# Dense relative-bias tables from the host, built with 16 transfers in place of 64, and the third modulation part accumulated at its place in the queue

## The chip, the core and the metric

The kernel runs on one core of a Trainium2 chip. The metric is the device time of one execution in microseconds, as the median of several executions. Engines are named as in the profile: PE (TensorE matmul), PEld (its weight load), DVE (VectorE), ACT (ScalarE), POOL (GpSimd), SP (SyncE, which issues most DMAs; SPq in rows).

## The reference, cut to what matters

Two transformer layers over 1024 grid tokens (16 rows of 64 columns) and 256 context tokens, width 1024. Layer 0 has 8 neighbourhood-attention heads and 8 grouped-query heads on one input projection; layer 1 is differential attention. Every layer has six modulation vectors per condition, and a SwiGLU FFN.

```python
m = jax.nn.silu(cond) @ w + b                 # six parts: sh1, sc1, g1, sh2, sc2, g2
h = modulate(rms_norm(x), sh1, sc1)           # h * (1 + scale) + shift
...
col_bias = rpb[:, :, col_idx - cols[:, None] + (WIN_C - 1)]
bias = jnp.take(col_bias, row_off, axis=1)    # 15 row offsets x 31 column offsets per head
s_win = einsum(q_r, k_win) * scale + bias     # 8 rows x 16 columns around the query
p = softmax(concat([s_win, s_ctx]))           # plus the 256 context keys
...
x = x + g1 * y
x = x + g2 * swiglu(modulate(rms_norm(x), sh2, sc2), ...)
```

The condition vectors are two: one for the latent tokens, one for the context tokens. The neighbourhood bias of a head is used dense over 64 key columns and 64 query columns, with -1e30 outside the 16-column window.

## The kernel before, in words

Every matmul on activations and weights is done in three passes of split operands (`mm3`, L181 to L183: high by high, low by high, high by low). `load_w` (L171 to L173) loads a weight chunk on SP, makes the high part on ACT and the low part on POOL or DVE.

**The first stage of layer 0**, where the change lies, runs up to the first attention matmul. After norm and the grouped-query projections it has two loops: the V projection (L665, two groups `g` of 10 token tiles) and the plain projections (L719, `ch` 0 to 7: 4 chunks of q, then 4 of k; each is 3 blocks of 24 matmuls into `psm` buffers, of which there are 4). `put_plain` (L360 to L364) evacuates each block on ACT and DVE, and the finished chunk is stored to DRAM (L729, L730).

Into both loops the program weaves side work:

- `maxima` (L408): for each head the row maxima of the scores, which the softmax uses later. A grouped-query head has 26 products (`qk`, L436) into `psq` buffers, of which there are 3, each followed by one DVE reduction (L414), and one transpose (L475). `early` (L650) hands out 200 steps of this over the two loops; the rest runs beside the attention.
- `tables(i, h)` (L626): eight calls, for `i` in (key table, query table) and four pairs of heads. Each does two parts: two broadcast loads of a row of the bias to 64 partitions (L634), one POOL add of the column mask `cmt` (L635), two stores to the DRAM table `sk` (L638). A row of the table has 127 columns, so that `skew` (L151) can read the 64 wanted ones of each row offset from a shifted start. `key_table` (L797, L798; tile TT) and `query_tables` (L813, L814; TQ, TG) read these rows back, in runs of 64 floats.
- the modulation vectors: `ada_acc` (L203) loads eight 128x1024 blocks of one of the six parts (`aw`, L207) and accumulates them for both conditions on DVE (2 x L210, then 14 x L214). `ada_sum` (L230) sums over partitions with 16 single-column matmuls (L235) into a `psq` buffer and adds the bias (L238). Three parts are done here, (0,2), (0,3) and (0,4): summed at the head of V group 1, after chunk 1, and after chunk 4.

The tile `aw` has 3 buffers, and the tables use the same tag: loads of table parts and of modulation blocks take turns in them, in the program's order.

**The order of the work.** A list scheduler puts the instructions of each engine in one fixed order; on the chip each engine and each DMA queue works in that order and waits at its head. `later()` (L298) lowers the priority of what it encloses by 3000, so that it falls behind other ready work. Table calls and all three `ada_acc` stand under `later()`.

Behind the first stage comes the attention of layer 0 (heads 8 to 15, then 0 to 7): `operands` loads q, k and V of each head (L770 to L788), `attend` makes the scores (L857, L858 into `pst`), the probabilities (ACT L847, L852, DVE L850, POOL and DVE L853) and the products with V (L892 to L895 into `psv`). Then follow output projection, FFN, and layer 1.

Of the kernel before, what the change touches and what calls it, by code (L numbers as in the profile page):

```python
# [9 lines left out]
F32 = mybir.dt.float32  # L10
# [7 lines left out]
P = 128  # L18
# [5 lines left out]
NFF = 22  # L24
EPS = 1e-6
GW = 64
RPW = 127
RPN = 15 * RPW
NEG = -1e30
LATER = 3000  # L30
AHEAD1 = 0.25
# [18 lines left out]


@with_exitstack
def kernel(ctx: ExitStack, tc: tile.TileContext, xT, cond, ada_w, ada_b, win0, wv0, wout0, rp, rpf, qg, kg,
                       win1, wv1, wout1, wg, wu, wd, lamv, subln, fgain, cosT, sinT, consts, cmT, cmQ, out):
    nc = tc.nc
    f = lambda ap: ap.bitcast(F32)
    uid = [0]

    def nm(s):
        uid[0] += 1  # L60
        return f"{s}_{uid[0]}"
# [15 lines left out]
    def order(a, b):  # L77

        tc.add_manual_dep(b.ins, a.ins.name, mybir.DependencyInfo(mybir.DependencyClass.NoSync, mybir.DependencyReason.DATA),
                          reason="activation table")  # L80
# [36 lines left out]
    def dram(shape, name):  # L117
        return dpool.tile(shape, F32, name=name)
# [10 lines left out]
    ls1 = dram([8, 2, 2, 8, P], "ls1")  # L129
    xs = dram([KD, P, NX], "xs")  # L130
    onesrow = dram([2, NT], "onesrow")
    sk = [dram([8, 64 * RPN + 2048], f"sk{i}") for i in range(2)]

    def small_operands():
        nc.sync.dma_start(slt, subln)
# [13 lines left out]
        nc.vector.tensor_scalar(slt, slt, 1.0 - LAMBDA_INIT, None, op0=ALU.mult)  # L149

    def skew(i, h, dr0, n):  # L151
        o = 63 + dr0 * RPW
        v = sk[i][h, o : o + 64 * (RPN - 1)].rearrange("(c n) -> c n", c=64)
        return v[:, : n * RPW].rearrange("c (u y) -> c u y", y=RPW)[:, :, :GW]


    pq = [None]
# [18 lines left out]
    def load_wchunk(src, eng=None):  # L176
        hi, lo = load_w(src, eng=eng, view=("p (k m) -> p k m", dict(k=KD)))
        return hi.rearrange("p (k m) -> p k m", k=KD), lo.rearrange("p (k m) -> p k m", k=KD)
# [6 lines left out]
    def project(o, w, hh, hl, ks=tuple(range(KD)), between=None):  # L185
        for i, k in enumerate(ks):
            mm3(o, w[0][:, k, :], w[1][:, k, :], hh[k], hl[k], k == ks[0], k == ks[-1])
            if between:
                between((i + 1) / len(ks))
# [13 lines left out]
    def ada_acc(pool, l, mod, conds, behind=None):  # L203
        acc = [pool.tile([P, 1024], F32, tag="acc", bufs=2, name=nm("acc")) for _ in range(conds)]
        for k in range(KD):
            w = pool.tile([P, 1024], F32, tag="aw", bufs=3, name=nm("aw"))
            nc.sync.dma_start(w, ada_w[l, k, :, mod * 1024 : (mod + 1) * 1024])  # L207
            for c in range(conds):
                if k == 0:
                    ins = nc.vector.tensor_scalar(acc[c], w, cs[:, k, c : c + 1], None, op0=ALU.mult)  # L210
                    if behind:
                        order(behind, ins)
                else:
                    nc.vector.scalar_tensor_tensor(acc[c], w, cs[:, k, c : c + 1], acc[c], op0=ALU.mult, op1=ALU.add)  # L214
        return l, mod, acc
# [82 lines left out]
    def later():  # L298

        return tc.high_priority(-LATER)  # L300
# [82 lines left out]
    def t5(pool, dt=F32R):  # L383
        return pool.tile([P, NT], dt, tag="t5", bufs=T5[0], name=nm("t5"))
# [104 lines left out]
    with sbuf("hp0", 8) as hp, sbuf("a10", 8) as ap:  # L489
# [31 lines left out]
        adas = [(0, 2, 2), (0, 3, 2), (0, 4, 2)]  # L521
# [86 lines left out]
        for g in range(2):  # L608
            w1 = load_wchunk(win0[8 + 2 * g], None if g else nc.vector)
            w2 = load_wchunk(win0[9 + 2 * g], None if g else nc.vector)  # L610
            o = [(t5(tpool), t5(tpool)) for _ in range(2)]
# [8 lines left out]
            for blk in BLK0:  # L620
                if g == 0:
                    gqa_k(wk, hi, lo, blk)
                gqa_q(g, w1, w2, o, blk)
        cmt = ap.tile([P, 2, RPW], F32, tag="cmt", bufs=1, name="cmt")

        def tables(i, h):  # L626

            for d0, d1 in ((0, 8), (8, 15)):
                n = d1 - d0
                T = ap.tile([P, 8, RPW], F32, tag="aw", bufs=3, name=nm("sk"))[:, 0:n, :]  # L630
                T2 = T.rearrange("p u y -> p (u y)")
                for j in range(2):
                    src = (rpf, rp)[i][h + j : h + j + 1, d0 * RPW : d1 * RPW].to_broadcast([64, n * RPW])
                    nc.sync.dma_start(T2[64 * j : 64 * j + 64], src)  # L634
                nc.gpsimd.tensor_add(T, T, cmt[:, i : i + 1, :].to_broadcast([P, n, RPW]))  # L635
                for j in range(2):
                    dst = sk[i][h + j, : 64 * RPN].rearrange("(c n) -> c n", c=64)[:, d0 * RPW : d1 * RPW]
                    nc.sync.dma_start(dst, T2[64 * j : 64 * j + 64])  # L638

        mpool = None  # L640
        tabs8 = [(i, h) for h in range(0, 8, 2) for i in range(2)]
# [1 line left out]
        def next_tables():  # L643
            with later():
                tables(*tabs8.pop(0))
# [4 lines left out]
        def early(x):  # L650

            nonlocal done0
            while done0 < EARLY0 * x and next(side0, "end") != "end":
                done0 += 1
# [6 lines left out]
        with later():  # L661
            pend_ada = ada_acc(ap, *adas.pop(0), last_sub[0])
        tok = [(0, i * P) for i in range(2)] + [(1, i * P) for i in range(4)] + [(2, i * P) for i in range(4)]

        for g, (v0, vw, pr0) in enumerate(((0, 384, 0), (384, 256, 3))):  # L665
# [53 lines left out]
        for ch in range(8):  # L719
            w = load_wchunk(win0[ch])  # L720
            hi, lo = t5(tpool), t5(tpool)
            for b, c0, cw, _ in BLK0:
                pst = mmt()[:, :cw]
                project(pst, w, hh[b], hl[b])
                early(VSHARE + (1 - VSHARE) * (ch * 1280 + c0 + cw) / 10240)
                put_plain(pst, hi[:, c0 : c0 + cw], lo[:, c0 : c0 + cw], 0.125 if ch < 4 else None)
            r = slice(P * (ch % 4), P * (ch % 4) + P)
            q = nc.gpsimd if ch > 6 else nc.sync
            q.dma_start((qh0, kh0)[ch // 4][r], f(hi))  # L729
            q.dma_start((ql0, kl0)[ch // 4][r], f(lo))  # L730
            if ch < 4:
                next_tables()
            if ch in (1, 4):
                ada_sum(*pend_ada, qmt)
            if ch == 1:
                with later():
                    pend_ada = ada_acc(ap, *adas.pop(0))

        stack0.close()

# [391 lines left out]
    with sbuf("hp1", 8) as hp:  # L1132
# [39 lines left out]
        with sbuf("a11", 8) as ap, psum("pa11") as pq[0]:  # L1172
# [12 lines left out]
            with sbuf("a11r", 8, side="right") as rpool:  # L1185
# [4 lines left out]
                for g in range(4):  # L1190
                    for kind in (1, 0):
                        w1 = load_wchunk(win1[kind * 8 + 2 * g], None if g or not kind else nc.vector)
                        w2 = load_wchunk(win1[kind * 8 + 2 * g + 1], None if g or not kind else nc.vector)
                        o = [(t5(ap), t5(ap)) for _ in range(2)]
                        for b, c0, cw, ci in BLK0[1:] + BLK0[:1]:
# [6 lines left out]
                            dst = [(x[:, c0 : c0 + cw], y[:, c0 : c0 + cw]) for x, y in o]  # L1202
# [7 lines left out]
                        for e in range(4):  # L1210
                            for j in range(2):
                                for i in range(2):
                                    src = f(o[j][i][32 * e : 32 * e + 32])
                                    r = (4 * g + e) * P + 32 * j + 64 * (1 - i if kind else i)
                                    nc.sync.dma_start((ks1 if kind else qs1)[r : r + 32, :], src if kind else src[:, NCTX:])
            vpool = stack.enter_context(sbuf("a11v", 4, side="right"))
            for g in range(2):
# [12 lines left out]
                for t in range(10):  # L1230
                    b, o = tok[t]
# [250 lines left out]
```

## Time and profile before

| | us |
|---|---|
| median of 3 executions | 3731.78 (3731.51 to 3735.49) |
| profiled execution, its own time | 3735.98 |
| its span in the profile | 3734.2 |
| busy: PE | 3443.2 (92%) |
| busy: DVE | 2313.8 (62%) |
| busy: ACT | 1420.3 (38%) |
| busy: POOL | 978.8 (26%) |

Durations are taken from the one profiled execution; all positions are microseconds from the start of its span. [...] A busy PE is not a PE at its peak, and consecutive matmuls overlap: their pace is read from their starts.

### The profile page before, as it was taken

Reading aid. Unit: us, or ns where it says so; the run is one execution under the profiler, and the core shown is the slowest. Engines: PE = TensorE matmul, PEld = TensorE weight load, DVE = VectorE, ACT = ScalarE, POOL = GpSimd, SP = SyncE. Lnnn points to the kernel's source line nnn. Section 1 sums busy time; section 2 is a strip of 40 time slices with the busy share of each in tenths; the row PEclk is TensorE's granted clock in tenths of the full one; section 3 lists DMA queues with packets and bytes.
Section 4 is the critical chain, followed back from the end, with each engine's and each line's share of the span. In section 5 each row is a group of like instructions: output and inputs, shape, how many; then the busy total and the mean of one; then the engine's idle time right before and its main releaser. Section 6 shows DMA issues by size and latency. Waiting matters only on the chain.

```text
span 3734.2 us, 43534 instructions
## 1 busy us (share of the span) xinstructions
PE 3443.2 (92%) x16044; PEld 2810.3 (75%) x16044; DVE 2313.8 (62%) x3530; ACT 1420.3 (38%) x2720; POOL 978.8 (26%) x702
## 2 busy tenths in 40 slices
PE   6799699988999999999998898998888999999997
PEld 4688477766888888888886677886666788888886
DVE  7777488887745555553337466879999643433335
ACT  4431077666431111111115355985555531111112
POOL 3212177664210000000003230006666200000002
PEclk8899699998999999999999999998888999999999
DMA  5377764375322332230113546455331311111111
GB/s 208 83 250 221 207 124 99 87 142 149 113 68 85 108 96 91 85 108 34 40 40 96 151 134 166 148 163 139 106 105 41 133 51 51 46 51 50 46 45 62
DMA packets 198079, 394.49 MB, mean 106 GB/s; under 512 B 57692, under 2 KB 99216, under 8 KB 197866
## 3 DMA queue, kind: packets, MB, share of 16 engines
q1 hardware_dynamic: 196074, 388.62, 35.7%
q0 software_dynamic: 1792, 3.10, 0.2%
q8 instruction: 126, 2.06, 0.2%
q14 instruction: 87, 0.71, 0.1%
HBM read 317.03 MB, written 74.61 MB: 105 GB/s over the span
## 4 chain that ended last, share of the span: by engine, by line
PE 68%; DVE 16%; issue 5%; ACT 4%; POOL 3%; DMA 3%; SPq 1%; POOLq 0%; DVEq 0%; ACTq 0%
PE psd L181 6%; PE psd L182 6%; PE psd L183 6%; PE psg L181 5%; PE psg L182 5%; PE psg L183 5%; PE psu L183 4%; PE psu L182 4%; PE psu L181 4%; PE psm L183 4%; PE psm L182 4%; PE psm L181 4%; DVE ph L1336 3%; DVE e L1335 2%; PE psq L1067 2%
## 5 line engine op out<-in xcount | busy, mean ns | idle before, releaser
L173 POOL TENSOR_TENSOR wl<-wr,wh 128x1024 fp32r<-128x1024 f32 x69 | 167.9, 2434 | 1525.1 <-ACT wh L172 1254.6
L172 ACT CAST wh<-wr 128x1024 fp32r<-128x1024 f32 x193 | 202.2, 1048 | 763.3 <-PE psd L182 305.3
L997 DVE SCALAR_TENSOR_TENSOR x<-psd,mods,x 128x512 f32<-128x512 f32 (+1 forms) x448 | 301.2, 687 | 185.1 <-PE psd L183 185.0
L1031 DVE TENSOR_TENSOR sg<-sg,psu 128x512 f32<-128x512 f32 (+1 forms) x110 | 69.7, 634 | 484.1 <-PE psu L183 481.9
L181 PE MATMUL psd<-ah,wh 128*128 128x512 f32 (+1 forms) x896 | 330.1, 369 | 9.7 <-DVE x L997 7.5
L182 PE MATMUL psd<-al,wh 128*128 128x512 f32 (+1 forms) x896 | 327.9, 366 | 0.0
L183 PE MATMUL psd<-ah,wl 128*128 128x512 f32 (+1 forms) x896 | 326.6, 365 | 0.6 <-DVE wl L173 0.6
L181 PE MATMUL psg<-hh,wh 128*128 128x512 f32 (+1 forms) x880 | 326.2, 371 | 0.1
L183 PE MATMUL psg<-hh,wl 128*128 128x512 f32 (+1 forms) x880 | 325.1, 369 | 0.6 <-DVE wl L173 0.6
L182 PE MATMUL psg<-hl,wh 128*128 128x512 f32 (+1 forms) x880 | 324.8, 369 | 0.0
L183 PE MATMUL psu<-hh,wl 128*128 128x512 f32 (+1 forms) x880 | 323.9, 368 | 0.6 <-POOL wl L173 0.5
L181 PE MATMUL psu<-hh,wh 128*128 128x512 f32 (+1 forms) x880 | 324.0, 368 | 0.0
L182 PE MATMUL psu<-hl,wh 128*128 128x512 f32 (+1 forms) x880 | 323.6, 368 | 0.0
L173 DVE TENSOR_TENSOR wl<-wr,wh 128x1024 fp32r<-128x1024 f32 x124 | 155.0, 1250 | 215.6 <-ACT wh L172 195.6
L1337 POOL TENSOR_TENSOR pl<-e,ph 128x512 fp32r<-128x512 f32 x160 | 255.0, 1598 | 119.9 <-DVE ph L1336 69.4
L1069 DVE TENSOR_REDUCE st<-psq 128x1 f32<-128x512 f32 (+1 forms) x384 | 219.5, 596 | 57.8 <-PE psq L1068 53.0
L1070 ACT ACTIVATE psq<-psq,st 128x512 f32<-128x512 f32 (+1 forms) x384 | 226.8, 594 | 64.5 <-DVE st L1069 60.8
L181 PE MATMUL psm<-hh,wh 128*128 128x512 f32 (+1 forms) x584 | 218.1, 374 | 26.2 <-ACT wh L172 18.7
L853 POOL TENSOR_TENSOR pl<-sb,ph 128x512 fp32r<-128x512 f32 (+1 forms) x144 | 202.5, 1413 | 96.0 <-ACT ph L852 63.4
L182 PE MATMUL psm<-hl,wh 128*128 128x512 f32 (+1 forms) x584 | 217.4, 373 | 7.0 <-DVE hl L353 5.4
L183 PE MATMUL psm<-hh,wl 128*128 128x512 f32 (+1 forms) x584 | 218.2, 374 | 3.8 <-POOL wl L173 3.8
L1332 ACT ACTIVATE e<-pst 128x1024 f32<-128x1024 f32 x160 | 163.5, 1026 | 129.7 <-PE pst L1330 66.5
(277 smaller groups left out, 8438.5 us busy)
## 6 DMA issues: line engine op xcount, KB each, us to landing
aw<-in_ada_w SPq DMA_DIRECT2D x112, 512.0 KB
wr<-in_wg SPq DMA_DIRECT2D x44, 512.0 KB
wr<-in_wu SPq DMA_DIRECT2D x44, 512.0 KB
wr<-in_wd SPq DMA_DIRECT2D x44, 512.0 KB
k<-ks SPq DMA_DIRECT2D x32, 640.0 KB
wr<-in_wout SPq DMA_DIRECT2D x32, 512.0 KB
q<-qs SPq DMA_DIRECT2D x32, 512.0 KB
k<-ks SPq DMA_DIRECT2D x48, 320.0 KB
```

Source lines behind the costliest of these rows:

```text
L172: nc.scalar.copy(hi, raw)
L173: (eng or nc.gpsimd).tensor_sub(lo, raw, f(hi))
L181: nc.tensor.matmul(o, ah, bh, start=start, stop=False)
L182: nc.tensor.matmul(o, ah, bl, start=False, stop=False)
L183: nc.tensor.matmul(o, al, bh, start=False, stop=stop)
L853: (nc.vector if npb[0] % LOD == 0 else nc.gpsimd).tensor_sub(lo, e, f(hi))
L997: nc.vector.scalar_tensor_tensor(xv, pst, mods[:, l, ci, 40 + oc : 41 + oc], xv, op0=ALU.mult, op1=ALU.add)
L1069: nc.vector.tensor_reduce(st[:, 0, a, j : j + 1], p1, axis=AX.X, op=ALU.max, negate=True)
L1070: after_table(nc.scalar.activation(p1, p1, AF.Exp, bias=st[:, 0, a, j : j + 1], accum_out=st[:, 1, a, j : j + 1]))
L1332: after_table(nc.scalar.activation(e, pst, AF.Exp))
L1336: nc.vector.tensor_copy(hi, p)
L1337: nc.gpsimd.tensor_sub(lo, p, f(hi))
```

## The change

It does three things.

1. The host lays the bias out dense, as two arrays of 8 x 64 rows by 15 x 64 columns (`tabT`, `tabQ`), each row already shifted to its column. A call of `tables` is now one 128x960 load, one POOL add, and one 128x960 store. Counted in the program, 64 DMA instructions (32 L634, 32 L638) and 16 POOL adds become 16 and 8. The DRAM tables hold 960 columns a row, and `skew` reads the row offsets that it wants as one contiguous run.
2. The `ada_acc` of part (0,4) no longer stands under `later()`.
3. The `ada_sum` of part (0,4) comes after chunk 6 in place of chunk 4.

```diff
-    sk = [dram([8, 64 * RPN + 2048], f"sk{i}") for i in range(2)]
+    sk = [dram([8 * 64, 15 * GW], f"sk{i}") for i in range(2)]
...
     def skew(i, h, dr0, n):
-        o = 63 + dr0 * RPW
-        v = sk[i][h, o : o + 64 * (RPN - 1)].rearrange("(c n) -> c n", c=64)
-        return v[:, : n * RPW].rearrange("c (u y) -> c u y", y=RPW)[:, :, :GW]
+        return sk[i][64 * h : 64 * h + 64, dr0 * GW : (dr0 + n) * GW].rearrange("c (u y) -> c u y", y=GW)
...
         def tables(i, h):
-            for d0, d1 in ((0, 8), (8, 15)):
-                n = d1 - d0
-                T = ap.tile([P, 8, RPW], F32, tag="aw", bufs=3, name=nm("sk"))[:, 0:n, :]
-                T2 = T.rearrange("p u y -> p (u y)")
-                for j in range(2):
-                    src = (rpf, rp)[i][h + j : h + j + 1, d0 * RPW : d1 * RPW].to_broadcast([64, n * RPW])
-                    nc.sync.dma_start(T2[64 * j : 64 * j + 64], src)
-                nc.gpsimd.tensor_add(T, T, cmt[:, i : i + 1, :].to_broadcast([P, n, RPW]))
-                for j in range(2):
-                    dst = sk[i][h + j, : 64 * RPN].rearrange("(c n) -> c n", c=64)[:, d0 * RPW : d1 * RPW]
-                    nc.sync.dma_start(dst, T2[64 * j : 64 * j + 64])
+            T = ap.tile([P, 15, GW], F32, tag="aw", bufs=3, name=nm("sk"))
+            r = slice(64 * h, 64 * h + P)
+            nc.sync.dma_start(T.rearrange("p u y -> p (u y)"), (tabT, tabQ)[i][r])
+            nc.gpsimd.tensor_add(T, T, cmt[:, i : i + 1, :].to_broadcast([P, 15, GW]))
+            nc.sync.dma_start(sk[i][r], T.rearrange("p u y -> p (u y)"))
...
-            if ch in (1, 4):
+            if ch in (1, 6):
                 ada_sum(*pend_ada, qmt)
             if ch == 1:
-                with later():
-                    pend_ada = ada_acc(ap, *adas.pop(0))
+                pend_ada = ada_acc(ap, *adas.pop(0))
```

The mask `cmt` shrinks from 127 to 64 columns with it. Line numbers of the changed program are lower by 3 in this region, by 10 in the attention.

The scheduler moves other work with these edits. Three places follow; numbers behind a name tell buffers apart.

**PE, at the end of the projections.** `psm_3652` (before) and `psm_3588` (changed) are the last block of chunk 7; `acc` are the accumulators of part (0,4) for the two conditions; `psq<-km,qm` are products of `maxima`; `pst` is the first score of the attention. Before, the last projection matmul is followed by the sum of part (0,4) and then by 52 products and 2 transposes of `maxima` ahead of the first `pst`:

```order
L183 MATMUL psm_3652<-hh_543,wl_3556 128x512
L235 MATMUL psq_3240<-cst,acc_2734 128x1 x8
L436 MATMUL psq_3292<-km_1366,qm_2901 128x512
L436 MATMUL psq_3295<-km_1366,qm_2901 128x256
L235 MATMUL psq_3240<-cst,acc_2735 128x1 x8
L436 MATMUL psq_3298<-km_1366,qm_2901 128x512
L436 MATMUL psq_3328<-km_1366,qm_2901 128x512
L436 MATMUL psq_3331<-km_1366,qm_2901 128x256
```

In the changed program:

```order
L180 MATMUL psm_3588<-hh_543,wl_3492 128x512
L433 MATMUL psq_3613<-km_1366,qm_3311 128x512
L433 MATMUL psq_3616<-km_1366,qm_3311 128x256
L433 MATMUL psq_3619<-km_1366,qm_3311 128x512
L433 MATMUL psq_3622<-km_1366,qm_3311 128x512
L433 MATMUL psq_3625<-km_1366,qm_3311 128x256
L433 MATMUL psq_3628<-km_1366,qm_3311 128x512
L433 MATMUL psq_3631<-km_1366,qm_3311 128x512
L433 MATMUL psq_3692<-km_1366,qm_3311 128x256
L433 MATMUL psq_3695<-km_1366,qm_3312 128x512
L847 MATMUL pst_3699<-t_726_3677,t_728_3683 128x256
```

The sum (now L232) has moved into the first two blocks of chunk 7, and 43 of the 52 products stand between the matmuls of chunks 3 to 7; 9 are left behind the last projection matmul.

**SP, the loads of part (0,4).** `aw` are its eight blocks, `sk_NN<-sk_NNNN` stores of table parts, `sk<-in_...` loads of them. Before, the eight loads stand behind the operands of the first three heads of the attention and behind the sixth table:

```order
L773 DMA t_851_4138<-qm_88 1x1280
L638 DMA sk_99<-sk_2703 64x1016
L638 DMA sk_99<-sk_2709 64x889 x2
L207 DMA aw_2736<-in_ada_w 128x1024
L207 DMA aw_2740<-in_ada_w 128x1024
L207 DMA aw_2744<-in_ada_w 128x1024
L207 DMA aw_2748<-in_ada_w 128x1024
L207 DMA aw_2752<-in_ada_w 128x1024
L207 DMA aw_2756<-in_ada_w 128x1024
L207 DMA aw_2760<-in_ada_w 128x1024
L207 DMA aw_2764<-in_ada_w 128x1024
L634 DMA sk_2924<-in_rpf 64x1016 x2
```

Now they stand behind the stores of chunk 1 (`ql<-t_491`), around the store of chunk 2 (`qh<-t_530`):

```order
L721 DMA ql_87<-t_491_2523 128x1280
L629 DMA sk_99<-sk_2362 128x960
L627 DMA sk_2512<-in_tabT 128x960
L627 DMA sk_2663<-in_tabQ 128x960
L204 DMA aw_2688<-in_ada_w 128x1024
L629 DMA sk_98<-sk_2512 128x960
L629 DMA sk_99<-sk_2663 128x960
L204 DMA aw_2692<-in_ada_w 128x1024
L204 DMA aw_2696<-in_ada_w 128x1024
L204 DMA aw_2700<-in_ada_w 128x1024
L425 DMA km_1366<-kh_89 64x1280
L204 DMA aw_2704<-in_ada_w 128x1024
```

The loads have gone ahead of the stores of chunks 2 to 6 and of all operands of the attention; the operands now follow the store of chunk 6.

**DVE, the accumulation of part (0,4).** Before, its 16 instructions stand as one run behind the last evacuation of chunk 7. Now the first two stand in chunk 2, and 14 stand here, between reductions of `maxima` (`mx<-psq`) and ahead of the evacuation of the first block of chunk 3 (three rows below the last one shown):

```order
L411 TENSOR_REDUCE mx_2858<-psq_2866 128x1
L211 SCALAR_TENSOR_TENSOR acc_2686<-aw_2692,cs,acc_2686 128x1024
L211 SCALAR_TENSOR_TENSOR acc_2687<-aw_2692,cs,acc_2687 128x1024
L211 SCALAR_TENSOR_TENSOR acc_2686<-aw_2696,cs,acc_2686 128x1024
L211 SCALAR_TENSOR_TENSOR acc_2687<-aw_2696,cs,acc_2687 128x1024
L211 SCALAR_TENSOR_TENSOR acc_2686<-aw_2700,cs,acc_2686 128x1024
L211 SCALAR_TENSOR_TENSOR acc_2687<-aw_2700,cs,acc_2687 128x1024
L211 SCALAR_TENSOR_TENSOR acc_2686<-aw_2704,cs,acc_2686 128x1024
L211 SCALAR_TENSOR_TENSOR acc_2687<-aw_2704,cs,acc_2687 128x1024
L411 TENSOR_REDUCE mx_2858<-psq_2869 128x1
```

Six more follow, then the reductions of `psq_2913`, `psq_2916` and `psq_2919`. On PE, counted in the same listing, 44 matmuls of 512 columns stand between the products `psq_2916` and `psq_2919`, and 3 of 512 and 24 of 256 columns between `psq_2919` and the next product; with three buffers, `psq_2919` needs the reduction of `psq_2869`, and the next product that of `psq_2913`. The run has moved from behind the projections to their first half; the accumulation of part (0,3) has moved ahead too, and is spread from V group 1 to chunk 2.

## Rows read from the trace of the kernel before

**Rows 1.** The chain that ended last, shares of the span by engine (page).

```profile
PE 68%; DVE 16%; issue 5%; ACT 4%; POOL 3%; DMA 3%; SPq 1%; POOLq 0%; DVEq 0%; ACTq 0%
```

**Rows 2.** Stretches: start:end, length, busy time by engine, granted clock, DMA share, GB/s.

```profile
240.00:404.00 164.00, 161.65 (x855) 139.45 (x855) 98.35 (x187) 28.23 (x78) 41.20 (x22) 0.94 0.70 218
404.00:438.40 34.40, 0.24 (x2) 0.04 (x1) 17.84 (x17) 0.58 (x1) 1.15 (x2) 0.57 0.83 254
438.40:473.70 35.30, 32.64 (x87) 21.83 (x88) 27.60 (x55) 0.53 (x2) 10.46 (x13) 0.50 0.63 166
460.00:480.00 20.00, 18.74 (x54) 12.55 (x54) 17.65 (x34) 4.98 (x10) 6.76 (x13) 0.57 0.93 204
473.70:935.00 461.30, 417.02 (x1898) 323.94 (x1897) 383.67 (x698) 326.52 (x614) 308.49 (x266) 0.96 0.53 117
```

**Rows 3.** PE in order of time: start, length, count, [idle before and releaser].

```profile
403.82 0.39 PE L183 MATMUL psm<-hh,wl 128*128 128x512 f32 x1
438.36 3.57 PE L235 MATMUL psq<-cst,acc 128*128 128x1 f32 x16 [34.16 <-DVE acc L214]
...
453.32 13.42 PE L436 MATMUL psq<-km,qm 128*128 128x256 f32 x26
...
473.63 0.41 PE L857 MATMUL pst<-t,t 128*128 128x256 f32 x1
```

**Rows 4.** DVE in order of time, 404 to 468 us.

```profile
404.86 0.69 DVE L361 TENSOR_TENSOR t<-psm,t 128x512 fp32r<-128x512 f32 x1 [4.75 <-ACT t L360]
420.69 1.42 DVE L210 TENSOR_SCALAR acc<-aw,cs 128x1024 f32<-128x1024 f32 x2 [15.14 <-DMA aw<-in_ada_w]
422.67 16.83 DVE L214 SCALAR_TENSOR_TENSOR acc<-aw,cs,acc 128x1024 f32<-128x1024 f32 x14 [0.57 <-DMA aw<-in_ada_w]
...
454.90 12.68 DVE L414 TENSOR_REDUCE mx<-psq 128x1 f32<-128x512 f32 x24 [0.23 <-PE psq L436]
```

**Rows 5.** SP's queue in order of time: issue times and lengths.

```profile
412.62 0.43 SPq L773 DMA_DIRECT2D t<-qm  x1
413.10 2.02 SPq L638 DMA_DIRECT2D sk<-sk  x3
415.16 17.52 SPq L207 DMA_DIRECT2D aw<-in_ada_w  x8
```

**Rows 6.** PE in order of time, full speed in chunk 7, 512 and 256 columns.

```profile
390.86 0.28 PE L183 MATMUL psm<-hh,wl 128*128 128x256 f32 x1
390.98 0.28 PE L181 MATMUL psm<-hh,wh 128*128 128x256 f32 x1
...
400.19 0.39 PE L182 MATMUL psm<-hl,wh 128*128 128x512 f32 x1
400.42 0.39 PE L183 MATMUL psm<-hh,wl 128*128 128x512 f32 x1
```

**Rows 7.** PE in order of time around the sum of part (0,3).

```profile
325.81 1.95 PE L235 MATMUL psq<-cst,acc 128*128 128x1 f32 x16 [0.88 <-DVE acc L214]
...
328.98 2.25 PE L235 MATMUL psq<-cst,acc 128*128 128x1 f32 x16
331.08 0.77 PE L183 MATMUL psm<-hh,wl 128*128 128x512 f32 x1
331.66 0.63 PE L436 MATMUL psq<-km,qm 128*128 128x512 f32 x1
...
337.15 0.39 PE L183 MATMUL psm<-hh,wl 128*128 128x512 f32 x1
```

**Rows 8.** POOL, then DVE, in order of time: an overlap of the two.

```profile
318.03 2.73 POOL L173 TENSOR_TENSOR wl<-wr,wh 128x1024 fp32r<-128x1024 f32 x1 [13.62 <-ACT wh L172]
...
317.22 1.28 DVE L214 SCALAR_TENSOR_TENSOR acc<-aw,cs,acc 128x1024 f32<-128x1024 f32 x1
...
319.08 2.76 DVE L214 SCALAR_TENSOR_TENSOR acc<-aw,cs,acc 128x1024 f32<-128x1024 f32 x1
```

**Rows 9.** DMA issues of the page: out<-in, engine, count, KB each.

```profile
sk<-sk SPq DMA_DIRECT2D x16, 254.0 KB
...
sk<-sk SPq DMA_DIRECT2D x16, 222.2 KB
```

**Rows 10.** The key tables (tile TT): what ended idle time before their users.

```profile
POOL TT L800: 4.3, 2
...
POOL TT L801: 2.6, 4
DMA TT<-sk: 0.5, 1
```

More of the change, by code (lines that the diff above doesn't have):

```diff
@@ L26 @@
 GW = 64
-RPW = 127
-RPN = 15 * RPW
 NEG = -1e30
@@ L52, with kernel @@
 @with_exitstack
-def kernel(ctx: ExitStack, tc: tile.TileContext, xT, cond, ada_w, ada_b, win0, wv0, wout0, rp, rpf, qg, kg,
+def kernel(ctx: ExitStack, tc: tile.TileContext, xT, cond, ada_w, ada_b, win0, wv0, wout0, tabT, tabQ, qg, kg,
                        win1, wv1, wout1, wg, wu, wd, lamv, subln, fgain, cosT, sinT, consts, cmT, cmQ, out):
@@ L623 @@
                 gqa_q(g, w1, w2, o, blk)
-        cmt = ap.tile([P, 2, RPW], F32, tag="cmt", bufs=1, name="cmt")
+        cmt = ap.tile([P, 2, GW], F32, tag="cmt", bufs=1, name="cmt")
         def tables(i, h):
-            for d0, d1 in ((0, 8), (8, 15)):
-                n = d1 - d0
-                T = ap.tile([P, 8, RPW], F32, tag="aw", bufs=3, name=nm("sk"))[:, 0:n, :]
-                T2 = T.rearrange("p u y -> p (u y)")
-                for j in range(2):
-                    src = (rpf, rp)[i][h + j : h + j + 1, d0 * RPW : d1 * RPW].to_broadcast([64, n * RPW])
-                    nc.sync.dma_start(T2[64 * j : 64 * j + 64], src)
-                nc.gpsimd.tensor_add(T, T, cmt[:, i : i + 1, :].to_broadcast([P, n, RPW]))
-                for j in range(2):
-                    dst = sk[i][h + j, : 64 * RPN].rearrange("(c n) -> c n", c=64)[:, d0 * RPW : d1 * RPW]
-                    nc.sync.dma_start(dst, T2[64 * j : 64 * j + 64])
+            T = ap.tile([P, 15, GW], F32, tag="aw", bufs=3, name=nm("sk"))
[3 more added lines that the diff above has]
+            nc.sync.dma_start(sk[i][r], T.rearrange("p u y -> p (u y)"))
         mpool = None
@@ L1419 @@
     rp = np.pad(inp["na_rpb"][0], ((0, 0), (0, 0), (48, 48)))
+    x = GW - 1 - np.arange(GW)[:, None] + np.arange(GW)[None, :]
+    tabQ, tabT = (t[:, :, x].transpose(0, 2, 1, 3).reshape(8 * GW, 15 * GW) for t in (rp, rp[:, ::-1, ::-1]))
     qgain, kgain = inp["gqa_q_gain"][0], inp["gqa_k_gain"][0]
@@ L1435 @@
     inside = (c[None, :] >= start[:, None]) & (c[None, :] < start[:, None] + 16)
-    x = np.arange(RPW)
-    kc = np.clip(c[:, None] + x[None, :] - 63, 0, GW - 1)
-    mq = np.where(inside[c[:, None], kc], f32(0), f32(NEG)).astype(f32)
-    qc = np.clip(c[:, None] + x[None, :] - 63, 0, GW - 1)
-    mt = np.where(inside[qc, c[:, None]], f32(0), f32(NEG)).astype(f32)
-    cmT, cmQ = np.concatenate([mt, mt], axis=0), np.concatenate([mq, mq], axis=0)
+    mq = np.where(inside, f32(0), f32(NEG)).astype(f32)
+    cmT, cmQ = np.concatenate([mq.T, mq.T], axis=0), np.concatenate([mq, mq], axis=0)
     arrays = dict(
@@ L1451 @@
         wout0=chunks(inp["par_w_out"][0], np.arange(D)),
-        rp=rp.reshape(8, RPN), rpf=rp[:, ::-1, ::-1].reshape(8, RPN),
+        tabT=tabT, tabQ=tabQ,
         qg=np.stack([np.tile(qgain[0::2], 4), np.tile(qgain[1::2], 4)], axis=1),
```

## The prediction, as put on record before the changed kernel had run

> **What bounds the kernel now.** I read the chain that ended last first, then busy time by stretch around the edited loops, and then the instructions of PE, DVE and SP in order of time. The chain lies on PE for 68% of the span, on DVE for 16% [rows 1]: work taken off another engine is worth something only where PE waits for it. By stretch [rows 2], PE is busy 161.65 of 164 us from 240 to 404, at a granted clock of 0.94, while DVE is busy only 98.35. Then it stops: 0.24 us of 34.4 up to 438.4. [...]
>
> PE's own rows [rows 3] say what the hole is. The last projection matmul ends at 404.2. The next instruction is the sum of part (0,4), after 34.16 us of idle time that ended with DVE's accumulation. Behind it stand 52 products of `maxima` and 2 transposes, and the first score starts at 473.63. So 473.6 - 404.2 = 69.4 us hold no projection and no attention. DVE [rows 4] is late because it idles 15.14 us for the load of the first block; its 16 accumulations then end at 439.5. And SP [rows 5] issues these loads only from 415.16, behind operands of the attention and a table's stores. The wait is one of order: loads that need nothing stand late in SP's queue, while DVE had room in the 164 us before.
>
> **Part 1, the accumulation and its sum.** All 69.4 us are taken away, and what was in them comes back elsewhere:
>
> - *Products between projections.* By the order, 43 of the 52 products now stand between matmuls of chunks 3 to 7. Full-speed matmuls follow each other every 0.12 us at 256 columns and 0.23 at 512 [rows 6]. Of 26 products 16 have 512 and 10 have 256 columns: 16 x 0.23 + 10 x 0.12 = 4.9, so 0.186 each, and 43 cost 8.0 us.
> - *Nine products left behind the last projection matmul.* They are paced by their reductions, 12.68 / 24 = 0.53 us each [rows 4]: 4.8 us.
> - *The sum in chunk 7.* The one for part (0,3) had the same surroundings [rows 7]: its two groups of 16 matmuls take 1.8 and 2.1 us, 3.9 together. Behind it matmuls of 512 columns run at half pace from 331.1 to 337.0, so 3.0 of those 6 us are lost.
> - *Attention's start.* The clock of 460 to 480 is 0.57 [rows 2], so the first scores, up to about 477, still run at half pace. Without the hole this returns some 1.8 us.
> - *The new block on DVE.* 14 accumulations now stand ahead of the first evacuation of chunk 3. One takes 1.28 us alone [rows 8], so 17.9. Before it DVE may wait for the second block's load; the old run waited 0.57 for it [rows 4], and with projections' own loads in the queue I take 2. PE does not stop at once: between the last product that has a buffer and `psq_2919` lie 44 matmuls of 512 columns (10.1 us; some of 256 stand ahead of them, so 10.4), and 3 of 512 and 24 of 256 (3.6) before the next. That hides 14.0, and 2 + 17.9 - 14.0 leaves about 6 us of stall. A stop of PE was followed by half pace in [rows 7], so I add the same 3.0. Bounds: no stall, if the loads are in time and projections hide the rest; and 12 us of load waits (two loads of about 6, since the first accumulation started 420.69 - 415.16 = 5.5 us after the issue) with three collisions of 1.5 (below): 12 + 17.9 + 4.5 - 14.0 = 20.4, about 21.
> - *Operands of the attention.* Before, the hole hid the loads of the first heads; now they follow the store of chunk 6 and have some 25 us. The old loads had their turn while the queue was 0.83 and 0.63 busy [rows 2]. A slip is bounded by 0 and 10 us (two load times and the two issue times around them); I take 2, since most of the 69 us of cover was not used.
>
> DVE has room: 98.35 us, 16 accumulations of 1.2 (19.4), and 43 reductions of 0.53 (22.8) are 140.6 us of about 188 up to the new end.
>
> The sum: 69.4 - 8.0 - 4.8 - 3.9 - 3.0 + 1.8 - 6 - 3 - 2 = 40.5 us saved.
>
> **Part 2, the tables.** Old stores were 16 of 254.0 and 16 of 222.2 KB [rows 9], so 7.6 MB, and as much was loaded: 15.2 MB. Now 8 tables of 128 x 960 floats (480 KB) pass each way, 7.9 MB. At the 218 to 254 GB/s of these stretches 7.3 MB are 29 to 34 us of queue time. But the DMA engines were busy 164 x 0.70 + 34.4 x 0.83 + 35.3 x 0.63 = 166 us of the 234, and PE waited for them only through the order told above. With the 30 us taken off, some 136 us of work stand in about 193: room, so I price the edit at nothing there. What hides it is PE's projections; were they gone, it would be a few of those 30 us. [...] In the attention the reads become runs of 256 bytes times the row offsets instead of 256 bytes each; idle time that table reads caused is 4.3 + 2.6 on POOL and 0.5 on DMA [rows 10]. So the bound there is 0 to 7.4 us of gain; I take 0, since POOL is busy only 308 of 461 us [rows 2].
>
> [...] The accumulation beside POOL shows a price: DVE's row took 2.76 us in place of 1.28 while a POOL subtraction of 2.73 us ran [rows 8], so each such meeting costs about 1.5 us. [...] It speaks against moving accumulation to where weights are still being split: with three such meetings in the block, as in its upper bound, the sum would be 36.0 saved in place of 40.5. I count none in the sum, since of the 22 POOL instructions of 240 to 404 [rows 2] few can fall into one block of 18 us.
>
> **The rivals.**
>
> - *A new wait in the old one's place.* The block on DVE stalls by its upper bound of 21 and the operands slip by 10: 40.5 - 15 - 8 = 17 us saved, about 3715. For it: eight loads of 512 KB now stand in SP's queue ahead of later weight chunks, at a DMA share of 0.70 [rows 2]. Against it: DVE ran the old block with one wait of 0.57 [rows 4].
> - *More than that.* Neither stall nor its clock loss nor the slip comes (11 us more), and all 7.4 of the tables' waits go: 40.5 + 11 + 7.4 = 59 us, about 3673. For it: the DMA queue loses 30 us. Against it: with 14 accumulations in a row something must show.
> - *Slower: loads one at a time.* The second block's load stands on SP behind two stores of tables, and each tile `aw` is shared with tables. Should only one load be under way at a time, each of the seven blocks costs DVE a load and 2.6 us of accumulation ahead of an evacuation. A load took about 6 us by itself; beside chunk weights it takes up to twice that, and at 8 the block is 7 x (8 + 2.6) = 74 us. 14 are hidden, so PE stands still for 60, and 3 of low clock follow, against the 49.5 that the other terms save: 13.5 slower, about 3745. It decides from a blocked time of 60.5 us, and shows as slower from 68. Against it: the old loads, all issued in 17.5 us [rows 5], fed 16 accumulations in 19 us.
> - *The change does not do what it says.* The hole is not due to order: the first head's operands or the tables would hold the attention at nearly the same time even with PE free. Then less than 7.5 us is saved, about 3729. Against it: operands are issued before 412.62 [rows 5] and PE did nothing else than `maxima` up to the first score.
>
> **How the numbers follow.** The profiled execution took 3735.98 us, 4.2 above the median of the three; the sum holds for either, so the forecast is 3731.78 - 40.5 = 3691. Its own range runs from no stall, clock loss or slip beyond the sum's other terms (51.5 saved, 3680) to the full stall (25.5 saved, 3706). Chances: forecast 0.70, new wait 0.14, more 0.06, slower 0.05, no difference 0.05. The range of 3670 to 3712 takes in the forecast's own, the larger gain and the nearer third of the new wait: about 0.80. A measurement of this kernel can tell 0.2%, which is 7.5 us, from no change. The forecast, the larger gain and the new wait all lie beyond that: faster 0.90, same 0.05, slower 0.05.
>
> **What would show it.** Right: idle time before the sum of part (0,4) falls from 34.16 to under 5 us; the last projection matmul comes later, near 428, and the first score earlier, near 435; the clock from 404 to 435 is near 1 instead of 0.5; PE waits some 6 us at a product in chunk 3, released by DVE; bytes moved fall by 7.3 MB; nothing past the first attention heads changes its length. Wrong: waits of DVE on `aw` of more than 6 us inside the block, PE idle for operands `t` at the first heads, projections that wait for weights behind the eight loads, or a time over 3720.

## The result, and the profile of the changed kernel

The changed kernel takes 3687.69 us (median of four, 3684.85 to 3688.74); the kernel before took 3732.53 beside it. The ratio is 0.9877 (95% interval 0.986 to 0.9894), 44.8 us less. The forecast was 3691, with 40.5 saved. The number held. The experiments show that the prediction put it down to the wrong part of the change.

The profiled executions are 3687.0 and 3734.2 us in span. Busy time by stretch of the changed kernel, with the columns of [rows 2] (length; PE, weight load, DVE, ACT, POOL; granted TensorE clock as a share of full speed, DMA share, GB/s):

```profile
240.00:404.00 164.00, 152.98 (x799) 130.58 (x798) 130.13 (x223) 27.18 (x77) 39.26 (x25) 0.92 0.62 214
404.00:440.00 36.00, 34.63 (x178) 27.51 (x177) 22.60 (x46) 4.24 (x9) 1.85 (x4) 1.00 0.74 199
440.00:935.00 495.00, 449.07 (x2129) 355.57 (x2129) 412.63 (x721) 335.64 (x628) 320.63 (x276) 0.98 0.48 124
```

Where PE did 0.24 us of work and then ran at a clock of 0.50, it is now busy 34.63 of 36 us at 1.00. DVE carries 32 us more in the stretch up to 404. PE of the changed kernel in order of time, the counterpart of [rows 3]:

```profile
357.89 0.38 PE L433 MATMUL psq<-km,qm 128*128 128x256 f32 x1 [3.84 <-DVE mx L411]
...
360.32 0.63 PE L179 MATMUL psm<-hl,wh 128*128 128x512 f32 x1
...
413.95 1.84 PE L232 MATMUL psq<-cst,acc 128*128 128x1 f32 x16
415.66 0.37 PE L179 MATMUL psm<-hl,wh 128*128 128x256 f32 x1
...
417.61 1.84 PE L232 MATMUL psq<-cst,acc 128*128 128x1 f32 x16
419.32 0.47 PE L180 MATMUL psm<-hh,wl 128*128 128x512 f32 x1
...
431.18 0.40 PE L180 MATMUL psm<-hh,wl 128*128 128x512 f32 x1
...
435.04 0.39 PE L847 MATMUL pst<-t,t 128*128 128x256 f32 x1
```

The sum of part (0,4) has no idle time before it; it was 34.16 us. The last projection matmul ends at 431.58, the first score starts at 435.04 instead of 473.63: 38.6 us earlier. The largest new stop of PE is the 3.84 us at 357.89, which DVE ends; further up, three products of `maxima` wait 0.87, 0.47 and 1.25 us (at 272.70, 284.57 and 309.00), where before one waited 0.62. DVE around the stop, the counterpart of [rows 4]:

```profile
339.36 9.65 DVE L211 SCALAR_TENSOR_TENSOR acc<-aw,cs,acc 128x1024 f32<-128x1024 f32 x8
348.93 0.68 DVE L411 TENSOR_REDUCE mx<-psq 128x1 f32<-128x512 f32 x1
349.53 4.86 DVE L211 SCALAR_TENSOR_TENSOR acc<-aw,cs,acc 128x1024 f32<-128x1024 f32 x4
355.02 2.48 DVE L211 SCALAR_TENSOR_TENSOR acc<-aw,cs,acc 128x1024 f32<-128x1024 f32 x2 [0.64 <-DMA aw<-in_ada_w]
```

This is the run of 14 accumulations, 17.0 us, with one wait of 0.64 for a load. The eight loads go out between 320 and 350 (from 415 in [rows 5]):

```profile
320.14 0.33 SPq L204 DMA_DIRECT2D aw<-in_ada_w  x1
...
334.30 1.28 SPq L204 DMA_DIRECT2D aw<-in_ada_w  x3
...
344.25 5.11 SPq L204 DMA_DIRECT2D aw<-in_ada_w  x3
```

### The profile page after: what moved, and what is told of

Same layout as the page of the kernel before. It is cut to its first block, busy times and chain, and to the rows that moved or that the text cites. A ratio compares the mean times of both kernels' runs of the same rounds, so it can differ in the third digit from the quotient of the medians.

```text
span 3687.0 us, 43450 instructions
## 1 busy us (share of the span) xinstructions
PE 3421.9 (93%) x16044; PEld 2801.2 (76%) x16044; DVE 2316.0 (63%) x3530; ACT 1418.9 (38%) x2720; POOL 966.3 (26%) x694
## 2 busy tenths in 40 slices
DMA packets 160447, 386.68 MB, mean 105 GB/s; under 512 B 19036, under 2 KB 60560, under 8 KB 160234
## 4 chain that ended last, share of the span: by engine, by line
PE 68%; DVE 16%; issue 5%; ACT 4%; POOL 3%; DMA 3%; SPq 1%; POOLq 0%; DVEq 0%; ACTq 0%
PE psd L178 6%; PE psd L179 6%; PE psd L180 6%; PE psg L178 5%; PE psg L179 5%; PE psg L180 5%; PE psu L180 4%; PE psu L178 4%; PE psu L179 4%; PE psm L180 4%; PE psm L179 4%; PE psm L178 4%; DVE ph L1326 3%; DVE e L1325 3%; PE psq L1057 2%
## 5 line engine op out<-in xcount | busy, mean ns | idle before, releaser
L179 PE MATMUL psd<-al,wh 128*128 128x512 f32 (+1 forms) x896 | 328.7, 367 | 0.0
```

The lines of the kernel that those rows point to most:

```text
L179: nc.tensor.matmul(o, ah, bl, start=False, stop=False)
```

## The experiments

All times are medians; ratios are to the kernel before, run beside them on the same chip, with 95% intervals. Versions from different groups of runs are best compared by their ratios.

**Each part alone.** Only the dense tables (`e1_tables`); from the changed kernel:

```diff
-            if ch in (1, 6):
+            if ch in (1, 4):
                 ada_sum(*pend_ada, qmt)
             if ch == 1:
-                pend_ada = ada_acc(ap, *adas.pop(0))
+                with later():
+                    pend_ada = ada_acc(ap, *adas.pop(0))
```

> Only the dense tables; part (0,4) keeps its lowered priority and its sum after chunk 4. Theory of the prediction (the accumulation's own edit brings the gain, tables bring nothing on the path): about 3732, the wait of some 34 us before the sum of part (0,4) stays. Rival (the tables share three buffers and SP's queue with the accumulation's loads; 16 in place of 64 transfers let the loads go ahead by themselves): about 3686, since the listing has the sum inside the projections with 9 products left behind the last one, and no run of 14 accumulations that stalls PE, so some 4 to 6 us of stall and half pace less than the changed kernel, offset by whatever its earlier sum costs.

Measured: 3687.05, ratio 0.9869 (0.9856 to 0.9882). The tables alone bring all of it. The eight loads of part (0,4), still under the lowered priority, now go out on SP between 322 and 367 (the first and the last two are shown), and the sum of part (0,4) lies inside the projections without either edit of the accumulation:

```profile
322.14 0.33 SPq L204 DMA_DIRECT2D aw<-in_ada_w  x1
...
363.48 3.87 SPq L204 DMA_DIRECT2D aw<-in_ada_w  x2
```

```profile
381.81 1.84 PE L232 MATMUL psq<-cst,acc 128*128 128x1 f32 x16
387.02 1.95 PE L232 MATMUL psq<-cst,acc 128*128 128x1 f32 x16 [0.35 <-DVE acc L211]
...
432.65 0.39 PE L848 MATMUL pst<-t,t 128*128 128x256 f32 x1 [0.68 <-DVE mx L411]
```

The other two edits with the old tables (`e2_order`), from the kernel before:

```diff
-            if ch in (1, 4):
+            if ch in (1, 6):
                 ada_sum(*pend_ada, qmt)
             if ch == 1:
-                with later():
-                    pend_ada = ada_acc(ap, *adas.pop(0))
+                pend_ada = ada_acc(ap, *adas.pop(0))
```

> Only the other two edits, with the old tables: part (0,4) at its place, its sum after chunk 6. Theory of the prediction: most of the gain, about 3690 to 3700. Rival (tables hold the loads back): the listing still has the sum behind the last projection matmul, the last two loads behind operands of the second head and 18 products left; I expect a wait of 5 to 20 us before the sum in place of 34, and 3695 to 3715. If it came out at 3732, the edit of the accumulation would be worth nothing without the tables.

Measured: 3738.54, ratio 1.0009 (1.0 to 1.0017): nothing gained. Neither theory's number came, but the last case of the expectation: without the tables the accumulation's edits are worth nothing. PE, then POOL, then SP of this run in order of time:

```profile
434.98 3.57 PE L235 MATMUL psq<-cst,acc 128*128 128x1 f32 x16 [20.73 <-DVE acc L214]
...
480.62 0.80 PE L856 MATMUL pst<-t,t 128*128 128x512 f32 x1 [14.72 <-ACT sb L846]
...
486.84 0.58 PE L891 MATMUL psv<-ph,v 128*128 128x256 f32 x1 [3.71 <-DMA v<-vs]
```

```profile
459.28 4.02 POOL L635 TENSOR_TENSOR sk<-sk,cmt 128x1016 f32<-128x1016 f32 x2
...
473.33 4.08 POOL L635 TENSOR_TENSOR sk<-sk,cmt 128x1016 f32<-128x1016 f32 x2 [9.19 <-issue]
...
478.68 4.95 POOL L852 TENSOR_TENSOR pl<-sb,ph 128x512 fp32r<-128x512 f32 x4
```

```profile
465.30 6.54 SPq L634 DMA_DIRECT2D sk<-in_rp  x4
...
475.52 3.00 SPq L638 DMA_DIRECT2D sk<-sk  x4
478.57 1.91 SPq L787 DMA_DIRECT2D v<-vs  x2
```

The wait before the sum falls from 34.16 to 20.73, just above the rival's 5 to 20, and the first score starts at 451.56, 22 us earlier than before. But the tables that the accumulation has passed now stand at the start of the attention: POOL must do their masks (473.33) before the low parts of the probabilities (478.68), and the loads of V wait on SP behind the table stores. PE stops for 14.72 and 3.71 us. In the kernel before, POOL did masks of tables at 440.50 and 458.18, while PE was at the sum and the 52 products. The wait was moved, not removed.

**The two small edits beside dense tables.** The sum after chunk 4 (`e3_ch4`), from the changed kernel:

```diff
-            if ch in (1, 6):
+            if ch in (1, 4):
```

> The changed kernel with the sum of part (0,4) after chunk 4 as before. Theory: the place of the sum matters little once the accumulation is early; the listing has it 8 blocks before the end in place of 2. Between 3685 and 3693: the same 14 accumulations in a row and the same stall of about 4 us, and some 3 us more if half pace follows the sum there (it followed a sum that had waited 1.3 us, and not one that had not waited).

Measured: 3690.19, ratio 0.9877 (0.9863 to 0.989), as expected; its two groups at 377.01 and 380.57 took 1.84 us each, with the clock at 1.00 after both. The lowered priority kept (`e4_later`), from the changed kernel:

```diff
-                pend_ada = ada_acc(ap, *adas.pop(0))
+                with later():
+                    pend_ada = ada_acc(ap, *adas.pop(0))
```

> The changed kernel with the accumulation of part (0,4) under the lowered priority again (tables dense, sum after chunk 6). Theory of the prediction: with the lowered priority the loads are late again, 3720 to 3732. Rival (the tables alone free the loads): the listing spreads the 14 accumulations over four chunks between the evacuations, so PE has no stall of 3.8 us and no half pace after it: 3 to 7 us faster than the changed kernel, about 3683.

Measured: 3685.37, ratio 0.9868 (0.9853 to 0.9883). The rival is right about the wait: PE has no stop in chunks 3 and 4 and the first score starts at 424.64, 10.4 us before that of the changed kernel. In the profiled executions 3.4 of these are lost again up to the attention's last product with V, and 2.2 behind it; why was not looked for. In the end the median is only 2.3 us less, within the intervals. So the second edit brought no gain beside the tables, and the stall of 3.84 us came with it.

**What of the tables matters: bytes or transfers.** Dense, but 64 transfers of 64 rows and 16 adds, both other edits undone (`e7_dense64`); from the tables-alone kernel:

```diff
-            T = ap.tile([P, 15, GW], F32, tag="aw", bufs=3, name=nm("sk"))
...
+            for d0, d1 in ((0, 8), (8, 15)):
+                T = ap.tile([P, 8, GW], F32, tag="aw", bufs=3, name=nm("sk"))[:, 0:n, :]
...
+                for j in range(2):
+                    r = slice(64 * h + 64 * j, 64 * h + 64 * j + 64)
+                    nc.sync.dma_start(T2[64 * j : 64 * j + 64], (tabT, tabQ)[i][r, d0 * GW : d1 * GW])
```

> The dense tables, but in two parts a call and with transfers of 64 rows: 64 transfers and 16 POOL adds as before, 7.9 MB in place of 15.2 MB; lowered priority and sum after chunk 4 kept. Theory that the bytes count: near the dense tables with 16 transfers, 3686 to 3698. Theory that the number of transfers and adds counts: 3705 to 3732.

Measured: 3701.61, ratio 0.9899 (0.9882 to 0.9915): about four fifths of the gain. Here the loads of part (0,4) go out between 361 and 388. DVE waits 3.26 us for a block in the accumulation of part (0,3), and half pace follows PE's stop of 4.67:

```profile
288.27 4.61 DVE L211 SCALAR_TENSOR_TENSOR acc<-aw,cs,acc 128x1024 f32<-128x1024 f32 x2 [3.26 <-DMA aw<-in_ada_w]
```

The opposite cut, old bytes in 32 transfers, was tried first with a broadcast load (`e6_merged`, from the kernel before):

```diff
-                for j in range(2):
-                    src = (rpf, rp)[i][h + j : h + j + 1, d0 * RPW : d1 * RPW].to_broadcast([64, n * RPW])
-                    nc.sync.dma_start(T2[64 * j : 64 * j + 64], src)
+                src = (rpf, rp)[i][h : h + 2, d0 * RPW : d1 * RPW].unsqueeze(1).to_broadcast([2, 64, n * RPW])
+                nc.sync.dma_start(T2, src)
```

> The kernel before with one edit: the two loads of a table part are one load of 128 rows, the two stores one store; 32 transfers in place of 64, the same 15.2 MB, the same 16 POOL adds, lowered priority and sum after chunk 4 kept. Theory that the number of transfers is what held the accumulation's loads back: the listing has the sum 3 blocks before the end of the projections with 12 products left, and the time is near that of the dense tables, 3686 to 3698. Theory that the bytes are what counts: the loads wait in the queue, DVE waits for them and PE for DVE at the sum, 3705 to 3730.

Measured: 3930.41, ratio 1.051 (1.0494 to 1.0526). This run doesn't answer its question, since something else shows. While POOL waits for a load of 444.5 KB, the mean busy share of the 16 DMA engines is 0.13, at 51 GB/s:

```profile
430.00:448.00 18.00, 4.93 (x22) 3.87 (x21) 0.37 (x2) 0.59 (x1) 0.12 (x1) 0.69 0.13 51
```

```profile
447.88 1.93 POOL L634 TENSOR_TENSOR sk<-sk,cmt 128x889 f32<-128x889 f32 x1 [21.72 <-DMA sk<-in_rp]
```

That is the busy time of 2.1 engines (16 x 0.13). The load has two rows as its outer dimension, each repeated 64 times; that this form makes it slow was the author's estimate, which this run does not show. From 487 to 510, in a longer wait of POOL for such a load, the share is 0.29, with a store of chunk rows (`ql`, issued at 486.75) and a load of `aw` (498.23) beside it. So the same counts once more, with each row laid out 64 times by the host and plain blocks of 128 rows (`e8_rows128`). It also gives each pair of heads a DRAM table of its own (first two lines):

```diff
-    sk = [dram([8, 64 * RPN + 2048], f"sk{i}") for i in range(2)]
+    sk = [[dram([P + 2, RPN], f"sk{i}{j}") for j in range(4)] for i in range(2)]
...
+                nc.sync.dma_start(T2, (rpf, rp)[i][64 * h : 64 * h + P, d0 * RPW : d1 * RPW])
...
+                nc.sync.dma_start(sk[i][h // 2][0:P, d0 * RPW : d1 * RPW], T2)
```

> The merged transfers once more, in a form without a broadcast: the host lays out each table row 64 times, and load and store are plain blocks of 128 rows. 32 transfers in place of 64, 15.2 MB and 16 adds as before, lowered priority and sum after chunk 4 kept. The run before it with the same counts was 190 us slower, with a DMA share of 0.15 to 0.23 while POOL waited for a table: if that was the form of the transfer (two outer rows), this one is near the one with 64 dense transfers, 3690 to 3712. If bytes hold the loads back, 3715 or more and long waits of DVE for blocks; if the number of transfers does, 3690 and shorter waits than with 64 dense ones.

Measured: 3689.08, ratio 0.9872 (0.9855 to 0.9888), with the tables' bytes and 256-byte reads of before. Fewer transfers, each over all 128 rows, are enough for the whole gain (with the separate DRAM tables, which were not tried by themselves): the loads of part (0,4) go out between 353 and 377, with the 16 adds of before. They are not the only way to it, since half the bytes with 64 transfers brought four fifths.

Whether the bytes and the 256-byte runs cost anything beside fewer transfers, this run does not settle, though its time is that of the tables alone. Its projections end at 413.5, 15 us before those of `e1_tables` (428.6), but from the first score to the last product with V it takes 453.5 us in place of 441.0 (the clock of 420 to 450 is 0.67, and V comes late by 3.44 us). `e7_dense64`, with half the bytes, takes 454.2 there, and has 19804 packets under 512 bytes against 19036 in the changed kernel. What the two share is a call of `tables` in two parts, with 16 adds; that this is what lengthens the attention was not tried. Nor was how the scheduler weighs a transfer, so that either cut moves the accumulation ahead in its order.

**A faster version.** In the kernel before, the changed one and the first four versions, the sums of parts (0,2) and (0,3) wait 0.77 us or more and half pace follows, as in [rows 7]; that of part (0,4) in the changed kernel did neither. So the second sum was moved one chunk on (`v2_later26`), from `e4_later`; the accumulation of part (0,4) moves with it:

```diff
-            if ch in (1, 6):
+            if ch in (2, 6):
                 ada_sum(*pend_ada, qmt)
-            if ch == 1:
+            if ch == 2:
```

> The changed kernel with the lowered priority kept for part (0,4) and the sum of part (0,3) one chunk later (after chunk 2; the accumulation of part (0,4) follows it). In all kernels so far this sum waited 0.8 to 1.3 us for DVE and about 10 us of half pace followed, while the sum of part (0,4), which did not wait, kept full pace. In the listing DVE now ends the accumulation a block ahead of the sum. If the wait is what costs the clock: no half pace at this sum, 4 to 6 us faster than the version with the lowered priority, about 3680. If sums cost the clock in any case: no change, 3685.

Measured: 3676.3, ratio 0.9833 (0.9818 to 0.9848), 9 us less than `e4_later` by the medians and 13 by the ratios, more than expected. The sum, and busy time before, in and after it:

```profile
324.30 1.84 PE L232 MATMUL psq<-cst,acc 128*128 128x1 f32 x16
...
327.62 1.84 PE L232 MATMUL psq<-cst,acc 128*128 128x1 f32 x16
```

```profile
320.00:324.30 4.30, 4.30 (x30) 3.81 (x29) 2.78 (x7) 1.81 (x3) 4.30 (x3) 1.00 0.56 229
324.30:329.50 5.20, 5.20 (x44) 5.02 (x43) 1.95 (x6) 0.39 (x1) 2.30 (x2) 1.00 0.94 305
329.50:340.00 10.50, 10.50 (x48) 8.54 (x48) 6.62 (x13) 0.60 (x1) 0.00 (x0) 1.00 0.72 285
```

The sum of the changed kernel and the same stretch around it:

```profile
316.27 1.95 PE L232 MATMUL psq<-cst,acc 128*128 128x1 f32 x16 [1.32 <-DVE acc L211]
```

```profile
312.00:316.20 4.20, 2.95 (x14) 2.12 (x12) 4.13 (x4) 0.39 (x1) 2.26 (x1) 1.00 1.02 372
316.20:324.00 7.80, 7.73 (x39) 7.25 (x40) 2.51 (x6) 0.00 (x0) 2.56 (x2) 0.62 0.85 326
324.00:330.00 6.00, 6.00 (x19) 4.68 (x20) 2.66 (x6) 0.60 (x1) 1.85 (x1) 0.64 0.40 165
```

Then the first sum as well, with normal priority for part (0,2) and the sum four token tiles into V group 1 (`v9_sums_late`):

```diff
-        with later():
-            pend_ada = ada_acc(ap, *adas.pop(0), last_sub[0])
+        pend_ada = ada_acc(ap, *adas.pop(0), last_sub[0])
...
-            if g == 1:
-                ada_sum(*pend_ada, qmt)
...
             for t in range(10):
+                if g == 1 and t == 4:
+                    ada_sum(*pend_ada, qmt)
```

> As the version before, and the accumulation of part (0,2) at normal priority with its sum four token tiles into V group 1. If waits at sums cost the clock, the half pace after the first sum goes too: another 4 to 6 us, about 3675. Against it: DVE bounds the first 180 us, and 16 accumulations that go there at normal priority (19 us) may push that stage back: then 3685 to 3700.

Measured: 3678.86, ratio 0.9841 (0.9826 to 0.9855). Both sides of the expectation came: the clock of 240 to 350 is 1.00, and PE stops for 11.12 us at 195 behind the accumulations in V group 0. A priority lowered by 600 in place of 3000 spreads them (`w600_gap`):

```diff
-        pend_ada = ada_acc(ap, *adas.pop(0), last_sub[0])
+        with tc.high_priority(-600):
+            pend_ada = ada_acc(ap, *adas.pop(0), last_sub[0])
```

> A version with all three sums behind their accumulation by some work: part (0,2) at a priority lowered by 600 in place of 3000 with its sum four token tiles into V group 1, part (0,3) summed after chunk 2, part (0,4) after chunk 6. If a sum without a wait keeps the clock, there is no half pace from 240 to 260 either and no run of accumulations that stalls PE: 3 to 6 us faster than the version with only the second sum moved, about 3671. If the spread accumulations delay the evacuations of V: 3676 to 3685.

Measured: 3669.34, ratio 0.9819 (0.9802 to 0.9836), the lowest of all and clear of the changed kernel's interval; that of `v2_later26` overlaps with it. Its first sum still waits 0.16 us, and the clock falls to 0.50 from 245 to 255, behind it:

```profile
243.15 1.95 PE L232 MATMUL psq<-cst,acc 128*128 128x1 f32 x16 [0.16 <-DVE acc L211]
```

One token tile more (`w600_t5`):

```diff
-                if g == 1 and t == 4:
+                if g == 1 and t == 5:
```

> The version before with the first sum one token tile later (five in place of four). There it still waited 0.16 us and half pace followed from 245 to some 254. The listing has more evacuations of V between the accumulation and the sum now, but fewer between those of part (0,3). If a wait of 0.16 is enough to lose the clock and no wait is not: full pace at the first sum, 4 us gained; if the sum of part (0,3) now waits, some 5 us are lost there. Between 3662 and 3675.

Measured: 3678.19, ratio 0.9858 (0.9841 to 0.9874), above the expected range. Products of `maxima` ahead of the sum now wait, for 2.31 us at 250, and the sum itself 0.42 us.

## Why the prediction was right, and where it was not

- *The hole of 69.4 us.* Right: PE's wait at the sum was a matter of order, and it is gone. The first score was put near 435 and came at 435.04. The terms were read from the listing of the whole change, so they could come out although they were credited to the wrong edit.
- *Which edit does it.* Wrong. The step that failed is Part 2, "I price the edit at nothing", with the whole gain put under Part 1. The tables alone give 0.9869; the accumulation's edits alone give 1.0009. The text took the listing of the whole change and gave it to the edit that names the accumulation. The rows had hints of the other: SP issues the loads right behind three stores of tables [rows 5], and tables and blocks take turns in the same three buffers. Part 2 asked only whether the DMA queue has room for the bytes, not whether the transfers hold the loads back in the order. The loads of part (0,4) start to go out at 415 before, at 391 with the accumulation's edits alone, and at 322 with the tables alone. On the bytes the runs are divided: the one with all the old bytes in 32 transfers is as fast, but with 64 transfers half the bytes brought four fifths of the gain. The bytes moved fell by 7.8 MB (394.49 to 386.68), not 7.3: the KB of [rows 9] are of 1024 bytes.
- *Products between projections.* 8.0 forecast. From the first block of chunk 4 to the last projection matmul PE takes 77.5 us, before 58.3. Less the sum, the stall and its half pace (below), some 9.7 are left for the products and transposes moved there.
- *Products left behind the last projection.* 4.8 forecast; from 431.58 to 435.04 it is 3.5.
- *The sum.* 3.9 forecast, 3.4 measured (1.71 from start to start in each group). The 3.0 for half pace behind it did not come. The row that this was taken from [rows 7] had a wait of 0.88 before it.
- *The stall in the block.* 6 forecast, 3.84 and 0.21 measured: the block took 17.0 us (17.9 priced), and waited 0.6 for loads instead of 2. Its half pace (clock 0.62 from 358 to 362.5) costs about 2, where 3 were taken. The price of a meeting with POOL did not arise: no accumulation of the block was lengthened. In part (0,3) three were, ahead of the second sum: 3.13 us at 274.78 beside a POOL subtraction of 2.40, and one in each of two pairs, of 4.48 us at 303.87 and 4.41 at 313.00 (the pair at 355.02 took 2.48), beside additions of tables of 3.14 and 2.26. Why DVE is slower beside POOL no run shows.
- *Operands of the attention.* 2 forecast, none seen. The clock from 435 to 455 is 1.00, as the 1.8 for the attention's start had it.
- *What was not in the sum.* By the first block of chunk 4 the changed kernel is 8.2 us late (its evacuation starts at 354.09, before at 345.88). 1.9 of that is there at the first V matmul already, ahead of what moved on PE; in the rest are waits of 1.27, 1.44 and 1.32 us at the two earlier sums (1.45 and 0.88 before), 2.6 at products of `maxima` (0.6 before), and half pace behind the second sum, from 318 to 328.7 where it was 331.1 to 337.0. The terms that were put too high, some 10 us, hid this: that the number came so close is in part luck.
- *Behind the first score* another 8.6 us are gained in the pair of profiled executions. The attention up to its last product with V gives 4.7; the rest lies where PE's matmuls stand in the same order. From that product to the end the traces of the first-stage versions take from 2813 to 2818 us, so this part is the spread between executions. Whether longer table reads (bound 7.4 us, taken as 0) have a part in the 4.7 is open: the run that kept the short reads is as fast in all, but not in the attention.

So the forecast was right as to the hole and its size, by terms that were off on both sides, and wrong as to the edit that closes it. The rival of a new wait in the old one's place is what the accumulation's edits do without the tables; there DVE also waits for five of the loads, up to 6.19 us at 421.79. In the changed kernel the slower rival of single loads did not show: the block waited 0.64 us. That rival's time of up to twice 6 us for a load beside chunk weights was the author's estimate; a block that DVE waited for in part (0,3) was ready 6.1 us after its issue in the kernel before (294.69 to 300.75) and 7.9 in the run with 64 dense transfers (280.34 to 288.27).

## What to carry to other kernels

When one change holds several edits and the listing moves, list each edit alone before giving the move to one of them; the edit that names the moved instruction need not move it. Here loads that share buffers and a queue with other transfers came early when those others became fewer (or, for the most part, half as large); raising the loads' priority alone only pushed the others into the next stage. Leave some work on the waiting engine between an accumulation and the matmuls that sum it: here one chunk more ahead of the second sum gave 9 us by the medians.

## What the runs showed of the hardware

- A sum of 16 single-column matmuls did not by itself go with a lower clock. In fourteen pairs of sums of the first stage where neither group waited the clock stayed at 1.00 for the 10 us behind them. In every sum there that waited 0.16 us or more at full pace it fell to 0.50 for 3 to some 17 us. There is one exception: in the run with 64 dense transfers the sum at 325.10 did not wait, and half pace followed from 330 to 336. Nor did every wait go with a lower clock: behind the 1.25 us at 309.00 in the changed kernel it stayed at 1.00 up to the sum at 316. So half pace went with a sum that waited, but for one case whose cause is open, and why it did no run shows.
- Transfers of tables whose outer dimension has two entries, the loads among them broadcast, went with a DMA share of 0.13 (430 to 448, while only packets of tables moved) and a kernel that was 192 us slower than the one before (3930.41 and 3738.17). The same bytes in plain blocks of 128 rows did not: 3689.08, against 3736.38 for the kernel before beside it. Whether the broadcast or the two entries do it was not tried.
- The kernel before has 57692 packets under 512 bytes, the changed kernel 19036. The run with blocks of 128 rows keeps the tables' reads of 256 bytes, and its ratio is 0.9872, that of the tables alone 0.9869. As told above, the two differ by stretches, so this shows no cost of the packets and does not rule one out.
